# A two-layer recurrent trunk on one core: two low parts by GpSimd and a third buffer at the second layer's first sevenfold head, five low parts by accumulating DMA in the output projection's first pair

## The chip, the cores and the metric

The kernel runs on one core of a Trainium2 chip. The time is device microseconds of a whole execution. A profile is one execution that was recorded; its span runs from the first instruction to the last, and its own device time is a little longer than its span. Of the core's engines, PE multiplies matrices, DVE (VectorE), ACT (ScalarE) and POOL (GpSimd) work on rows of 128 partitions, SP issues most DMAs, and POOL issues those that add to what they write.

## What is computed

One inference step of a two-layer trunk, for a prompt of 1024 tokens and 32 sample tokens (together 1056 columns, D = 1024). Layer 0 is an RG-LRU block, layer 1 an HGRN2 block with 8 heads of 128. Cut to layer 1, on which the change works:

```
xn = _rmsnorm(x, g_norm)
u = xn @ w_in                       # 1024 x 4096: q, f, iv, gate
q, f, iv, gate = split(u, 4)
q = silu(q); log_g = log(lb + (1 - lb) * sigmoid(f)); k = 1 - exp(log_g); v = iv
o, S_T = chunked recurrence over q, k, v, log_g with state S0
o = o * rsqrt(mean(o * o) + EPS) * o_gain
y = o * silu(gate)
return x + y @ w_out, S_T           # then a final rmsnorm
```

All numbers are fp32. A product is taken on PE as three products of split operands: each number is cut into a high part `hi` (a rounded fp32r copy) and a low part `lo = x - hi`, and `hi hi + lo hi + hi lo` is summed in PSUM (lines 246, 247 and 248: one matmul each).

## The kernel before

The kernel is written as operations with reads, writes and an estimated duration, which a planner (`Flow`) puts in an order for each engine by list scheduling from both ends; each engine then runs its own list strictly in that order. So when one operation changes its engine or its estimate, the planner can reorder others near it.

**Products of layer 1.** Head 0 is projected plainly. From head 1 on (`HC = 1`), and in the output projection (`seven_out`), two output rows are computed together by a scheme of seven products (Strassen and Winograd) in place of eight: `seven(h, a, b, order)`. Each of the seven, here p1 to p7, is 24 matmuls of 264 columns: two halves x of 4 blocks of 3 matmuls (in `seven_out` 3 blocks, so 18). The string `order` is the order on PE: a digit is a product, "b" is a burst of the recurrence of the neighbouring head. The weights of the seven products come from four loaded blocks "11", "12", "21", "22" and a fifth buffer "s", combined in place by POOL (`combine`, L1467 for heads, L1677 for the output projection).

**Splitting a weight.** `split(p)` makes the high part by ACT (L1456, L1666) and the low part in one of two ways. `low` writes the negated high part by ACT (L319), and then POOL issues a DMA that adds the raw weight to it (L320). `subtract` computes raw minus high by DVE or by POOL (L333). Before, heads 1 to 6 use `low` for all seven, head 7 uses `subtract`, by POOL for p1, p2, p6, p7 and by DVE for the others, and the output projection uses `subtract` by DVE (`BYDMA` is empty). High and low parts have four buffers each (`NW = 4`), used in turn: p1 and p2 take two, the next two products of the order the other two, and a later product takes a buffer when PE has finished with it.

**Sums of x.** The seven products read x and sums of its rows. `build` makes p6, p7 and p4's sums (tiles `t2`, `t3`, `t4`, printed as `t`); `build1` makes p5's: for j = 0 to 3 it loads a row of xn (528 KB) into one of two spare buffers (`sg`, `a`), subtracts its halves (L1416), and splits the result into `xh` by ACT (L1379) and `xl` by DVE (L333). `build` also uses a third buffer, row 3 of `R`. Parts of that row hold weights of the next `seven`.

**The bursts.** Burst 3 of a head is 64 matmuls at L1061, which read rows that DVE has scaled at L1043 (`128x128x4`), and 64 at L1115, which read rows scaled next (`128x64x8`). Burst 4 reads rows scaled after those: L1139 (`128x32x16`) and L1146 (`128x16x32`). Each scaling comes in two instructions, one on `R` and one on `a` or `sg`. Burst 2 reads at L1061 rows scaled by `128x264x2`.

**Head 1 and the output projection.** Head 1's first `seven` runs in the order `FQ0`, with bursts 3 and 4 of head 0. The output projection runs four pairs of output rows, m = 0, 2, 4, 6, by `seven_out`; its operands are the sums of y (`youts`), split by ACT (L1626) and DVE (L333, tiles `xl` and `t`). Its first pair runs after head 7, whose burst 2 stands just before.

Of the kernel before, what the change touches and what calls it, by code (L numbers as in the profile page):

```python
# [24 lines left out]
NW, NXO, NRAW = 4, 3, 3  # L25
K1 = 6
NMM = 3
BYDVE, BYDMA = (1, 2, 3, 4, 5, 6, 7), ()
HC = 1
FQ0, FQ, GV = "1267b4b35", "12b675b43", "126b74b53"  # L30
SPOTS, SPOTS0 = (6, 9, 0, 2), (2, 5, -1, -1)
LAST = "12b675b43", "12b67b453", "12b675b43", "1b267543"
K2 = 8 - K1
# [7 lines left out]
TOK = SEQ + NB * NS  # L41
# [5 lines left out]
H = 8  # L47
# [167 lines left out]
def tile_trunk(ctx: ExitStack, tc: tile.TileContext, xT, prm, hc, w0, wg, wo0, w1, wo1, s_in,  # L215
               yT, h_out, c_out, sp_out, ss_out):
    nc = tc.nc
    V, S, G, T, Q = nc.vector, nc.scalar, nc.gpsimd, nc.tensor, nc.sync
# [11 lines left out]
    R = work.tile([128, 4, TOK], F32, tag="R", name="R")  # L230
# [70 lines left out]
    with ExitStack() as l0:  # L301
# [29 lines left out]
        def subtract(e, n, b, x, a, r, w, prio):  # L331

            emit = lambda: e.tensor_tensor(b, x, a.bitcast(F32), op=ALU.subtract)  # L333
            if e is G:
                pool(n, emit, r, w, prio)
            else:
                dve(n, emit, r, w, prio, True)
# [25 lines left out]
        rows = [C("sg") for _ in range(6)]  # L363
# [491 lines left out]
        raw = (halves[1][:8], [slots[i] for i in (1, 4, 7, 2, 5, 8)] + [halves[1][8], free[8]], free[:8])  # L855
# [82 lines left out]
    with ExitStack() as l1:  # L938
# [29 lines left out]
        SA = a_rows[1]  # L968
# [28 lines left out]
        def ykeys(m, a, n):  # L997

            return [("Y", m, i) for i, (u, v) in enumerate(zip(CUTS, CUTS[1:])) if u < a + n and v > a]
# [404 lines left out]

        def build1():

            spare = cycle([(rows[3], ykeys(1, 0, TOK)), (SA, [("SA", 0), ("SA", 1)])])
            for j in range(4):
                t, tk = next(spare)
                hk, lk = ([("T", 1, i, j, x) for x in range(2)] for i in (0, 1))  # L1410
                for i, ks_ in enumerate((hk, lk)):
                    for k in ks_:
                        inherit(k, [(("xh", "xl")[i], j, c) for c in (1, 2)])
                dma(t, xn[j], (), tk, 3, 528)
                t, o = t[:, :HT], t[:, HT:]
                dve(HT, lambda o=o, t=t: V.tensor_tensor(o, o, t, op=ALU.subtract), tk, tk, 3, True)  # L1416
                parted(HT, V, xh[j][:, HT:], xl[j][:, HT:], o, tk, hk, lk)
# [11 lines left out]
        def seven(h, a, b, order, at=()):  # L1429
# [24 lines left out]
            def split(p):  # L1454
                (raw, rk), (hi, hk), (lo, lk) = slot[named[p]], next(his), next(los)
                act(512, lambda: S.copy(hi, raw), (rk,), (hk,), 2)  # L1456
                if h < H - 1:
                    low(512, lo, raw, (rk,), (lk,), 2)
                else:
                    subtract(G if p in (1, 2, 6, 7) else V, 512, lo, raw, hi, (rk, hk), (lk,), 2)  # L1460
                parts[p] = hi, lo, (hk, lk)
                if p not in (1, 2):
                    freed.append(slot[named[p]])
# [28 lines left out]
            for c in order:  # L1492
# [5 lines left out]
                p = int(c)  # L1498
                if p == steps[-1]:
                    rawq = [moves.get(k, (o, k)) for o, k in freed]  # L1500
                hi, lo, wk = parts[p]
# [145 lines left out]
        def seven_out(m, order, at):  # L1647
# [15 lines left out]
            def split(p):  # L1663
                (raw, rk), (hi, hk), (lo, lk) = slot[named[p]], next(his), next(los)
                hi, lo = hi[:, :u], lo[:, :u]
                act(u, lambda: S.copy(hi, raw), (rk,), (hk,), 2)  # L1666
                if p in BYDMA:
                    low(u, lo, raw, (rk,), (lk,), 2)
                else:
                    subtract(V if p in BYDVE else G, u, lo, raw, hi, (rk, hk), (lk,), 2)  # L1670
                parts[p] = hi, lo, (hk, lk)
                if p not in (1, 2):
                    freed.append(whole[named[p]])
# [23 lines left out]
            for c in order:  # L1697
# [3 lines left out]
                p = int(c)  # L1701
                if p == steps[-1]:
                    rawq = [(o, k) for o, k in freed]
                hi, lo, wk = parts[p]
# [47 lines left out]
        for m in range(KD):  # L1752
            raw, rk = next(raws)
# [184 lines left out]
```

## Time and profile before

| | us |
|---|---|
| median of 3 runs | 1071.77 (1071.49 to 1074.11) |
| the profiled execution, its own time | 1068.75 |
| its span | 1067.0 |
| PE busy in the span | 1046.7 (98%) |
| DVE busy | 782.0 (73%) |
| ACT busy | 676.2 (63%) |
| POOL busy | 505.5 (47%) |

PE is busy in nearly all of the span, so the time is PE's work plus the little time in which it waits, or runs at a lower granted clock. The places of the change are read from PE's waits and from the order in time of DVE, ACT and POOL around them. A PE row in the order of time starts when its matmul starts, and its duration overlaps the next ones: starts of neighbours are 0.12 us apart at 264 columns.

### The profile page before, as it was taken

How to read it: one execution, taken by the hardware profiler on the slowest of the kernel's cores; microseconds unless marked ns; L12 is line 12 of the kernel's file. 1: busy time of each engine (PE TensorE's matmuls, PEld its weight loads, DVE VectorE, ACT ScalarE, POOL GpSimd, SP SyncE). 2: the span in 40 equal slices, each digit the busy share in tenths (PEclk: the TensorE clock that was granted, in tenths of full speed). 3: DMA queues.
4: the chain of work that ended last, by engine and by line, in shares of the span. 5: the costliest groups of instructions: out<-in, count | busy, mean ns of one | idle time of the engine just before them, and what ended most of it. 6: DMA issues, size and time to landing. Idle time of an engine off the chain costs nothing.

```text
span 1067.0 us, 25951 instructions
## 1 busy us (share of the span) xinstructions
PE 1046.7 (98%) x10120; PEld 1019.2 (96%) x10120; DVE 782.0 (73%) x1533; ACT 676.2 (63%) x1526; POOL 505.5 (47%) x528
## 2 busy tenths in 40 slices
PE   9999999999999999999989999999999989999997
PEld 9999999999999999999979999999999989999996
DVE  7999996888888688265786666656566576898636
ACT  6568656867765874243468685858586755865443
POOL 3425443454443456455544445455554454335354
PEclk9999999999999999999999999999999999999998
DMA  9111112124842685363685475756476652734634
GB/s 302 60 27 45 55 49 74 57 61 114 248 142 59 201 278 158 119 216 123 197 217 110 114 169 103 173 111 167 98 180 130 169 123 83 254 95 112 142 72 163
DMA packets 90331, 143.24 MB, mean 134 GB/s; under 512 B 11104, under 2 KB 55904, under 8 KB 90208
## 3 DMA queue, kind: packets, MB, share of 16 engines
q1 hardware_dynamic: 74656, 112.46, 33.2%
q0 software_dynamic: 13248, 26.35, 14.9%
q10 hardware_dynamic: 2304, 2.77, 0.8%
q8 instruction: 79, 1.29, 0.5%
q14 instruction: 44, 0.36, 0.1%
HBM read 81.60 MB, written 33.05 MB: 107 GB/s over the span
## 4 chain that ended last, share of the span: by engine, by line
PE 88%; DVE 7%; DMA 2%; ACT 1%; issue 1%; POOL 0%; POOLq 0%; ACTq 0%; SPq 0%; DVEq 0%
PE mm L246 24%; PE mm L248 24%; PE mm L247 24%; PE hg L1061 2%; PE hg L1278 1%; PE hg L577 1%; PE hg L1170 1%; PE hg L1280 1%; PE hg L1224 1%; PE hg L246 1%; PE hg L247 1%; PE hg L248 1%; DVE sg L1043 1%; DMA wlo<-wraw 1%; PE hg L1322 1%
## 5 line engine op out<-in xcount | busy, mean ns | idle before, releaser
L246 PE MATMUL mm<-xh,whi 128*128 128x352 f32 (+1 forms) x1147 | 354.7, 309 | 4.1 <-ACT os L1248 2.6
L247 PE MATMUL mm<-xl,whi 128*128 128x352 f32 (+1 forms) x1147 | 348.5, 304 | 0.0
L248 PE MATMUL mm<-xh,wlo 128*128 128x352 f32 (+1 forms) x1147 | 348.3, 304 | 0.0
L246 PEld LDWEIGHTS mm<-xh,whi 128*128 128x128 f32 x1147 | 215.5, 188 | 7.5 <-ACT os L1248 2.8
L247 PEld LDWEIGHTS mm<-xl,whi 128*128 128x128 f32 x1147 | 215.7, 188 | 1.7 <-issue 0.2
L248 PEld LDWEIGHTS mm<-xh,wlo 128*128 128x128 f32 x1147 | 215.6, 188 | 0.0
L333 POOL TENSOR_TENSOR wlo<-wraw,whi 128x512 fp32r<-128x512 f32 (+1 forms) x66 | 94.3, 1437 | 92.7 <-ACT whi L388 75.7
L248 PE MATMUL mm<-t,wlo 128*128 128x264 f32 x408 | 116.6, 286 | 3.8 <-DMA wlo<-wraw 3.8
L246 PE MATMUL mm<-t,whi 128*128 128x264 f32 x408 | 118.9, 291 | 0.0
L247 PE MATMUL mm<-t,whi 128*128 128x264 f32 x408 | 116.5, 286 | 0.0
L509 DVE SCALAR_TENSOR_TENSOR k<-xb,prm_sb,k 128x352 f32<-128x352 f32 (+2 forms) x144 | 90.1, 637 | 10.9 <-ACT k L506 6.1
L248 PEld LDWEIGHTS mm<-t,wlo 128*128 128x128 f32 x408 | 77.4, 190 | 4.2 <-DMA wlo<-wraw 4.2
L246 PEld LDWEIGHTS mm<-t,whi 128*128 128x128 f32 x408 | 77.6, 190 | 0.3
L247 PEld LDWEIGHTS mm<-t,whi 128*128 128x128 f32 x408 | 77.7, 190 | 0.1
L1540 DVE TENSOR_TENSOR k<-mm,k 128x264 f32<-128x264 f32 x72 | 30.6, 430 | 52.5 <-PE mm L248 50.4
L320 POOL DMA_DIRECT2D wlo<-wraw x51 | 44.5, 885 | 51.5 <-ACT wlo L319 35.6
L592 POOL TENSOR_TENSOR k<-X 128x352 f32<-128x352 f32 x36 | 43.8, 1226 | 47.6 <-DVE R L593 37.9
L246 PE MATMUL mm<-yh,whi 128*128 128x352 f32 x153 | 49.9, 326 | 0.0
L248 PE MATMUL mm<-yh,wlo 128*128 128x352 f32 x153 | 49.4, 323 | 0.0
L247 PE MATMUL mm<-yl,whi 128*128 128x352 f32 x153 | 49.4, 323 | 0.0
L388 ACT CAST whi<-wraw 128x512 fp32r<-128x512 f32 (+1 forms) x63 | 36.3, 591 | 20.2 <-DMA wraw<-in_w_dram 10.0
L320 POOL DMA_DIRECT2D wlo<-R x30 | 28.1, 936 | 43.1 <-ACT wlo L319 40.6
(425 smaller groups left out, 2724.2 us busy)
## 6 DMA issues: line engine op xcount, KB each, us to landing
wraw<-in_w_dram SPq DMA_DIRECT2D x88, 256.0 KB, 3.5
wlo<-wraw POOLq DMA_DIRECT2D x51, 256.0 KB, 4.0
wlo<-R POOLq DMA_DIRECT2D x30, 256.0 KB, 4.2
wraw<-in_wo_dram SPq DMA_DIRECT2D x37, 192.0 KB, 3.0
ysum<-sg SPq DMA_DIRECT2D x9, 528.0 KB, 4.0
si<-in_s_in_dram SPq DMA_DIRECT2D x8, 512.0 KB, 4.5
R<-in_w_dram SPq DMA_DIRECT2D x16, 256.0 KB, 3.3
out_ss_out_dram<-si SPq DMA_DIRECT2D x8, 512.0 KB, 2.7
```

Source lines behind the costliest of these rows:

```text
L246: T.matmul(out, wh, xh, start=first, stop=False, skip_group_check=chained)
L247: T.matmul(out, wh, xl, start=False, stop=False, skip_group_check=chained)
L248: T.matmul(out, wl, xh, start=False, stop=last, skip_group_check=chained)
L320: fl.add("POOL", 0.93, lambda: G.dma_start(dst.bitcast(F32), src, accum_op=ALU.add), (*r, *w), w, prio, n / 2)
L333: emit = lambda: e.tensor_tensor(b, x, a.bitcast(F32), op=ALU.subtract)
L388: act(m, lambda hi=hi, raw=raw, m=m: S.copy(hi[:, :m], raw[:, :m]), rk, (hk,), prio)
L509: dve(u, lambda src=src, dst=dst, sh=sh, k=k: V.scalar_tensor_tensor(dst, sh(src, k), pc("cw", 12 * k + m), dst, op0=ALU.mult, op1=ALU.add ...
L577: fl.add("PE", 0.62, lambda ps=ps, i=i, c=c: T.matmul(ps[:96, :CH], gs[:, i, :], ST[:96, chunk(c)], start=True, stop=True), (("gs",), *((" ...
L592: pool(CH, lambda x=x, a=a, b=b: G.tensor_tensor(x, a.bitcast(F32), b.bitcast(F32), op=ALU.add), (ak, bk), (xk,), 3)
L1043: dve(n // 2, lambda sv=sv, dv=dv, s=s, f=f: V.tensor_tensor(dv[:, :, s, :], sv[:, :, s, :], f, op=ALU.mult), (*sk, *gk), dk if i == o els ...
L1061: T.matmul(ps[32 * j:32 * j + 32, n * w:n * w + w], B[:, o:o + 32], q(slice(o, o + 32)), start=True, stop=True, tile_position=(0, 32 * j))
L1540: dve(QT, lambda: V.tensor_tensor(o[0], z[0], u[0], op=ALU.add), (z[1], u[1]), (o[1],), 0)
```

## The change

Head 1's first `seven` gets another order: p7 moves behind burst 3 (`FQ0`). In it, the low parts of p6 and p7 are made by POOL's subtraction in place of ACT's negated copy and POOL's adding DMA (`BYG`). `build1` gets row 3 of `R` as a third spare buffer. In the output projection's first pair (`MD = (0,)`), the low parts of p6, p7, p5, p4 and p3 are made by `low` in place of DVE's subtraction.

```diff
-BYDVE, BYDMA = (1, 2, 3, 4, 5, 6, 7), ()
+BYDVE, BYDMA, MD = (1, 2, 3, 4, 5, 6, 7), (6, 7, 5, 4, 3), (0,)
 HC = 1
-FQ0, FQ, GV = "1267b4b35", "12b675b43", "126b74b53"
+BYG = (6, 7)
+FQ0, FQ, GV = "126b74b35", "12b675b43", "126b74b53"
...
         def build1():
...
-            spare = cycle([(rows[3], ykeys(1, 0, TOK)), (SA, [("SA", 0), ("SA", 1)])])
+            spare = cycle([(rows[3], ykeys(1, 0, TOK)), (SA, [("SA", 0), ("SA", 1)]), (R[:, 3], [("R3", 0), ("R3", 1)])])
...
             def split(p):
...
-                if h < H - 1:
+                if h < H - 1 and ((h, a) != (HC, 0) or p not in BYG):
                     low(512, lo, raw, (rk,), (lk,), 2)
                 else:
-                    subtract(G if p in (1, 2, 6, 7) else V, 512, lo, raw, hi, (rk, hk), (lk,), 2)
+                    subtract(G if p in (1, 2, 6, 7) or h == HC else V, 512, lo, raw, hi, (rk, hk), (lk,), 2)
...
-                if p in BYDMA:
+                if m in MD and p in BYDMA:
                     low(u, lo, raw, (rk,), (lk,), 2)
                 else:
                     subtract(V if p in BYDVE else G, u, lo, raw, hi, (rk, hk), (lk,), 2)
```

One line is added near the top, so that line numbers of the changed kernel are one higher (L333 is L334 there). The texts name the lines of the kernel before, except in rows of the changed one.

**POOL in head 1.** This is POOL's list from the third combination of head 1's first `seven` on, before (`wraw_119` holds block "11" and then p6's weight, `wraw_120` p7's, `wraw_121` p4's, `kt_5251` p3's and later p5's; `wlo_126` and `wlo_127` are the low parts of p6 and p7):

```order
L1467 TENSOR_TENSOR wraw_119<-wraw_119,kt_5251 128x512
L1467 TENSOR_TENSOR kt_5251<-kt_5251,wraw_119 128x512
L320 DMA wlo_127<-wraw_120 128x512
L320 DMA wlo_126<-wraw_119 128x512
L320 DMA wlo_128<-wraw_121 128x512
L320 DMA wlo_129<-kt_5251 128x512
```

and the same place of the changed kernel:

```order
L1468 TENSOR_TENSOR wraw_119<-wraw_119,kt_5251 128x512
L1468 TENSOR_TENSOR kt_5251<-kt_5251,wraw_119 128x512
L334 TENSOR_TENSOR wlo_126<-wraw_119,whi_122 128x512
L334 TENSOR_TENSOR wlo_127<-wraw_120,whi_123 128x512
L321 DMA wlo_128<-wraw_121 128x512
L321 DMA wlo_129<-kt_5251 128x512
```

Two issues of adding DMAs (p7's first) are now two subtractions (p6's first), and p4's DMA stands behind them.

**DVE in head 1.** This is DVE's list from the first scaling for burst 3 on, before (`t41` is the low part of p4's sums, `sg_147`, `a_113` and row 3 of `R_73` are `build1`'s buffers, `k_85` takes sums from PSUM):

```order
L1043 TENSOR_TENSOR R_73<-R_73,sg_148 128x128x4
L1043 TENSOR_TENSOR sg_146<-sg_146,sg_148 128x128x4
L1043 TENSOR_TENSOR R_73<-R_73,sg_148 128x64x8
L333 TENSOR_TENSOR t41_5234<-a_113,t40_5233 128x1056
L1416 TENSOR_TENSOR sg_147<-sg_147 128x528
L1043 TENSOR_TENSOR a_112<-sg_146,sg_148 128x64x8
L1540 TENSOR_TENSOR k_85<-mm_156,k_85 128x264
L1540 TENSOR_TENSOR k_85<-mm_157,k_85 128x264
L333 TENSOR_TENSOR xl_94<-sg_147,xh_93 128x528
L1555 SCALAR_TENSOR_TENSOR R_73<-R_73,k_85 128x264
L1065 COPY_PREDICATED attnd_5236<-mask2_88,hg_162 128x256
L1065 COPY_PREDICATED attnd_5236<-mask4_89,hg_162 128x256
```

and in the changed kernel:

```order
L1044 TENSOR_TENSOR R_73<-R_73,sg_148 128x128x4
L1044 TENSOR_TENSOR sg_146<-sg_146,sg_148 128x128x4
L334 TENSOR_TENSOR t41_5234<-a_113,t40_5233 128x1056
L1044 TENSOR_TENSOR R_73<-R_73,sg_148 128x64x8
L1044 TENSOR_TENSOR a_112<-sg_146,sg_148 128x64x8
L1417 TENSOR_TENSOR sg_147<-sg_147 128x528
L1541 TENSOR_TENSOR k_85<-mm_156,k_85 128x264
L1044 TENSOR_TENSOR R_73<-R_73,sg_148 128x32x16
L1417 TENSOR_TENSOR R_73<-R_73 128x528
L334 TENSOR_TENSOR xl_94<-sg_147,xh_93 128x528
L1044 TENSOR_TENSOR a_112<-a_112,sg_148 128x32x16
L334 TENSOR_TENSOR xl_98<-R_73,xh_97 128x528
```

The scalings for burst 4 (`128x32x16`, and after these rows `128x16x32`) have come forward between the sums of `build1`, whose third sum now stands in `R`; the copies at L1065 and half of the sums from PSUM have gone behind them.

**DVE before the output projection.** This is DVE's list before burst 2 of head 7, before:

```order
L1043 TENSOR_TENSOR R_73<-R_73,ST_143 128x528
L1186 TENSOR_TENSOR kst_5242<-mm_156,kst_5242 32x128
L1186 TENSOR_TENSOR vst_5243<-mm_156,vst_5243 32x128
L1043 TENSOR_TENSOR a_112<-a_112,ST_143 128x528
L333 TENSOR_TENSOR xl_98<-xl_98,xh_97 128x528
L333 TENSOR_TENSOR xl_102<-xl_102,xh_101 128x528
L333 TENSOR_TENSOR xl_104<-xl_104,xh_103 128x528
L333 TENSOR_TENSOR xl_106<-xl_106,xh_105 128x528
L1043 TENSOR_TENSOR R_73<-R_73,sg_148 128x264x2
L1043 TENSOR_TENSOR sg_146<-a_112,sg_148 128x264x2
```

and in the changed kernel:

```order
L1044 TENSOR_TENSOR a_112<-a_112,ST_143 128x528
L1187 TENSOR_TENSOR kst_5242<-mm_156,kst_5242 32x128
L1187 TENSOR_TENSOR vst_5243<-mm_156,vst_5243 32x128
L1053 TENSOR_TENSOR sg_148<-ST_143 128x528
L1044 TENSOR_TENSOR R_73<-R_73,sg_148 128x264x2
L1044 TENSOR_TENSOR sg_146<-a_112,sg_148 128x264x2
L334 TENSOR_TENSOR xl_98<-xl_98,xh_97 128x528
L334 TENSOR_TENSOR xl_102<-xl_102,xh_101 128x528
L334 TENSOR_TENSOR xl_104<-xl_104,xh_103 128x528
L334 TENSOR_TENSOR xl_106<-xl_106,xh_105 128x528
```

The two scalings that burst 2 reads have moved ahead of four low parts of the sums of y.

On POOL, the five adding DMAs of the first pair stand among the combinations of its weights and two powers (L1306) of head 7's norms; on ACT, five negated copies are added in the same stretch. On SP, the load of `build1`'s third row (into `R`) stands ahead of the row for `a`, and the weight block that goes to row 3 of `R` has moved behind all four loads of `build1`.

## The prediction

> **What bounds the kernel now.** The page comes first: who is busy, and who ends the span.
>
> ```profile
> PE 1046.7 (98%) x10120; PEld 1019.2 (96%) x10120; DVE 782.0 (73%) x1533; ACT 676.2 (63%) x1526; POOL 505.5 (47%) x528
> ...
> PE 88%; DVE 7%; DMA 2%; ACT 1%; issue 1%; POOL 0%; POOLq 0%; ACTq 0%; SPq 0%; DVEq 0%
> ```
>
> PE bounds it, and the change adds and removes no matmul. So it can move the time only through PE's 20 us that are not busy, or through the granted clock. The view of PE's waits says where these are, and the windows give the clock there.
>
> ```profile
> PE mm L248 <- DMA wlo<-wraw: 3.8, 2, 3.5
> PE mm L246 <- ACT os L1248: 2.6, 1, 2.6
> PE hg L1061 <- ACT t L1626: 1.7, 1, 1.7
> ...
> 540.00:545.00 5.00, 2.16 (x18) 1.95 (x17) 5.00 (x8) 4.20 (x8) 1.71 (x3) 1.00 1.05 222
> 545.00:550.00 5.00, 4.31 (x23) 4.31 (x24) 3.31 (x8) 1.62 (x4) 0.65 (x1) 0.66 1.05 256
> 870.00:880.00 10.00, 7.25 (x176) 6.42 (x162) 8.70 (x13) 1.96 (x5) 9.40 (x9) 1.00 0.01 2
> ```
>
> The first and third waits lie in the two places of the change. The first costs more than its 3.5 us: behind it the clock column (third from the right) is 0.66 over 5 us, and 5 x 0.34 = 1.7 us of PE's work is lost on top. The second wait, in an unchanged place, cost no clock (1.00). In order of time, PE in head 1's first `seven`:
>
> ```profile
> 541.75 0.28 PE L246 MATMUL mm<-t,whi 128*128 128x264 f32 x1
> 541.88 0.28 PE L247 MATMUL mm<-t,whi 128*128 128x264 f32 x1
> 545.69 0.39 PE L248 MATMUL mm<-t,wlo 128*128 128x264 f32 x1 [3.53 <-DMA wlo<-wraw]
> ...
> 552.99 0.73 PE L1061 MATMUL hg<-R,sg 128*32 128x32 f32 x62
> 553.57 0.71 PE L1115 MATMUL hg<-R,a 128*16 128x16 f32 x62
> 554.21 0.39 PE L246 MATMUL mm<-t,whi 128*128 128x264 f32 x1
> 557.49 0.46 PE L1139 MATMUL hg<-R,a 128*32 128x32 f32 x32
> 558.78 0.69 PE L1146 MATMUL hg<-R,sg 128*64 128x64 f32 x16 [0.84 <-ACT wlo L319]
> 559.81 0.37 PE L246 MATMUL mm<-xh,whi 128*128 128x264 f32 x1
> 565.10 0.39 PE L246 MATMUL mm<-xh,whi 128*128 128x264 f32 x1 [0.37 <-DVE k L1540]
> ```
>
> At 541.75 p6 starts and at its third matmul waits for its low part. p7 follows, burst 3 (552.99), p4 (554.21), burst 4 (557.49), p3 (559.81), and p5, whose second half starts at 565.10. I compare that last moment.
>
> **Head 1: POOL's two subtractions.** Before, p6's low part was the second of these issues:
>
> ```profile
> 536.82 2.07 POOL L1467 TENSOR_TENSOR kt<-kt,wraw 128x512 f32<-128x512 f32 x1 [0.20 <-DMA wlo<-kt]
> 538.84 1.79 POOL L320 DMA_DIRECT2D wlo<-wraw  x2
> ...
> wlo<-wraw POOLq DMA_DIRECT2D x7, 256.0 KB, 4.8
> ...
> 871.55 1.27 POOL L333 TENSOR_TENSOR wlo<-wraw,whi 128x512 fp32r<-128x512 f32 x1
> 875.27 1.27 POOL L1467 TENSOR_TENSOR wraw<-wraw 128x512 f32<-128x512 f32 x1
> ...
> 871.92 5.17 DVE L1043 TENSOR_TENSOR sg<-sg 128x512 f32<-128x512 f32 x1
> ```
>
> An issue (0.9 us) and a landing (4.8) ended at 545.7. A subtraction of this very form took 1.27. POOL is free at 538.9, so p6's low part is there at 540.2, 1.8 us before PE asks, and p7's at 541.4. The 3.5 and the 1.7 us go; so do two negated copies on ACT and two transfers from a stretch whose DMA share was 1.05.
>
> What they cost falls on DVE. The last row shows it: a scaling that takes 0.69 elsewhere took 5.17, because POOL's subtractions and combinations ran without a gap from 871.55 to 876.54, and it ended 0.55 after them. DVE's list at the change, before:
>
> ```profile
> 537.66 2.35 DVE L333 TENSOR_TENSOR t<-R,t 128x1056 fp32r<-128x1056 f32 x1
> 539.98 1.26 DVE L1398 TENSOR_TENSOR a<-a,R 128x1056 f32<-128x1056 f32 x1
> 541.15 0.69 DVE L1043 TENSOR_TENSOR R<-R,sg 128x512 f32<-128x512 f32 x1
> 541.75 0.69 DVE L1043 TENSOR_TENSOR sg<-sg 128x512 f32<-128x512 f32 x1
> ...
> a<-xn SPq DMA_DIRECT2D x4, 528.0 KB, 5.5
> ...
> DMA to landing us min/median/max: 3.3/4.5/7.9
> ```
>
> The first row is 2.35 long because POOL held it until 538.9; 1.1 was left. Now POOL holds until 541.4, so it ends at 542.5, in time for p6's second half (541.75 + 12 x 0.12 = 543.2). Then, start to start, 1.2 for L1398 and 0.6 for each scaling: burst 3's first pair is ready at 544.9. `t41` (1.2) and the second pair (1.2) follow: 547.3.
>
> PE: p6 takes 24 x 0.122 = 2.9 us, to 544.65; L1061 starts at 545.0 and takes 0.6; L1115 **waits 1.8 us**, to 547.4, and ends at 548.05 (0.65, from its row to p4's). p7 and p4 end at 553.9. Burst 4 took 559.81 - 557.14 (p4's end, 554.21 + 2.93) = 2.67 with its wait of 0.84, so 1.8 without: p3 from 555.7.
>
> Is burst 4's input there? DVE after 547.3: two small steps, then scalings, sums and low parts of 0.6 in the order shown, to the last scaling at about 552.8. This needs the row of xn in `R`: its buffer is free at 543.7, and 5.5 us later, at 549.2, it has landed, just as DVE asks. L1146 asks 0.8 after burst 4 begins, at 554.7, so 1.9 us are spare; one operation of POOL fits. p5 needs the last `xl`, which stands behind p3's first half on DVE (555.7 + 1.45, then 0.45 + 0.35 + 0.6 and two hand-overs of 0.1): 558.8. Its second half starts 1.5 us later, at 560.3, against 565.10: **4.8 us gained**. The next `seven` begins earlier by the same; its first low parts now wait for PE's buffers, so they move with PE.
>
> Bounds. If POOL's three operations take 1.8 to 2.1 each, as L1467 at 536.82 did, 1.4 is lost; a landing of 7.9 (the longest of a low part's DMA there, the last row) in place of 5.5 costs 0.5 past the spare time, and some hand-overs 0.3. So 2.6 at least. With no wait at all it would be 4.8 + 1.8 + 0.4 = 7.0. I take the middle path, whose durations are rows of the same form.
>
> Of the clock: a wait of 2.6 kept 1.00 and one of 3.53 lost it, so 1.8 should keep it. The Trainium skill ("TensorE: Matmul & The Clock Gate", What's actually happening) says the clock halves after an idle window of about 3.4 us, and that the window runs free. The trace agrees. If every wait halved the clock, the sum would be 1.7 us worse.
>
> **Output projection: burst 2's wait.** PE waited 1.74 us for two scalings that stood behind four low parts:
>
> ```profile
> 932.18 0.75 PE L1061 MATMUL hg<-R,sg 128*32 128x32 f32 x64 [1.74 <-ACT t L1626]
> ...
> 927.40 3.40 DVE L333 TENSOR_TENSOR xl<-xl,xh 128x528 fp32r<-128x528 f32 x4
> 930.72 0.70 DVE L1043 TENSOR_TENSOR R<-R,sg 128x528 f32<-128x528 f32 x1
> 931.34 0.70 DVE L1043 TENSOR_TENSOR sg<-a,sg 128x528 f32<-128x528 f32 x1
> ...
> 952.13 0.39 PE L246 MATMUL mm<-t,whi 128*128 128x264 f32 x1
> 961.87 0.29 PE L246 MATMUL mm<-xh,whi 128*128 128x264 f32 x1
> ...
> 932.65 3.67 POOL L1677 TENSOR_TENSOR wraw<-wraw,R 128x384 f32<-128x384 f32 x1 [4.27 <-DVE wlo L333]
> 937.91 1.51 POOL L1677 TENSOR_TENSOR R<-R,wraw 128x384 f32<-128x384 f32 x1
> ...
> 950.00:960.00 10.00, 10.00 (x198) 9.43 (x197) 9.92 (x24) 7.05 (x25) 3.90 (x4) 1.00 0.29 81
> ...
> wlo<-wraw POOLq DMA_DIRECT2D x51, 256.0 KB, 4.0
> ```
>
> (ACT's `t` is named only because it came last; DVE's second scaling ended at 932.04.) With the four moved behind, the scalings start about 3 us earlier and end near 929, before PE's 930.4. So 1.7 goes, and the four low parts, which PE reads after 940, are hidden by p5 and p3.
>
> The five low parts themselves save DVE 5 x 0.5 us in a stretch where it is full (9.92 of 10), and cost POOL five issues of 0.9 and ACT five copies of 0.5, both with room (3.90, 7.05). Each lands 5 us after its copy: p6's near 945, and PE starts p6 (952.13 before) near 950.4. The tightest is p3's: its buffer is free when p6 ends, about 952.6, it lands near 958.5, and PE asks 1.7 earlier than 961.87, at 960.1. So they cost nothing as long as POOL comes to them. DVE's relief could also take away a later wait of 0.6 (968.09); bounds 0 to 2.3, and I take 1.7.
>
> **Sum.** 4.8 + 1.7 = 6.5 us: 1068.75 of the profiled execution becomes 1062.25. That execution was 3.0 below the median of the runs, so for the median 1071.77 - 6.5 = 1065.3.
>
> **Rivals.**
> 1. *The second gain is given back.* PE arrives at the next bursts earlier, with DVE as full as before, and waits there. For it: the row of 950 to 960. Only head 1's 4.8 is left: 1067.0.
> 2. *DVE becomes the bound in head 1.* POOL's run is longer, or the new row lands late, and burst 4 waits as well as burst 3; the gain is the lower bound of 2.6 with half of the second place, 0.9, or 1.3 less (one more operation of POOL) with none of it: 1068.3 to 1070.5. For it: the row of 5.17, and a DMA share above 1. Against it: two transfers of low parts are gone from that queue.
> 3. *Slower: POOL is starved before p6 of the first pair.* The row of 3.67 is a combination (1.27 x 384 / 512 = 1.0 alone) that waited while DVE ran without a gap. POOL's list is strict, and the adding DMAs of p6 and p7 stand behind the last such combination, which before needed no hurry. Were POOL held until 945.5, p6 would be just in time; each us later is a us of PE, and past 3.5 us the clock costs 1.7 more. From about 950 the whole gain of 6.5 is eaten, and at 955 the kernel is 4.7 slower: 1076.5. Against it: the row of 937.91, that last combination, which came through at once between DVE's operations that read PSUM. The Trainium skill speaks for it ("SBUF — State Buffer", SBUF: two separate sides): while DVE holds the port pair, POOL cannot write descriptors either. Here the row of 538.84 is against: two issues took 1.79 beside DVE's long operation.
> 4. *It doesn't do what it says*: the planner's order leaves p6 waiting. POOL's list rules it out.
>
> **How the numbers follow.** The forecast 0.62, rival 1 0.14, rival 2 0.16, rival 3 0.08. The lower end is both upper bounds, 7.0 + 2.3 = 9.3: 1062.5; the upper end takes in rival 2: 1070.5. About 0.3%, 3.2 us, is what a measurement can tell from no change: faster by more is the forecast and rival 1 (0.76), within it rival 2 (0.16), slower rival 3 (0.08).
>
> **What would show it.** Head 1: no wait on a low part at p6, a clock of 1.00 throughout, a wait of about 1.8 at L1115 for DVE's `a`, none or little at L1146, and two POOL rows of L334 near 1.3 each. Burst 2 of head 7: no wait at L1061. First pair: no wait on a DMA of `wlo`. It is wrong if L1115 or L1139 waits over 4 us, if the clock still falls, or if p6 or p3 of the first pair waits for its DMA.

## The result, and the profile after

The changed kernel takes 1065.74 us (median of 4 runs, 1063.54 to 1066.95), the kernel before, on the same chip, 1071.63 (4 runs). The ratio is 0.9955, 95% interval 0.9934 to 0.9976. A second measurement with more runs agrees: 1065.13 (12 runs) against 1069.36 (35 runs), ratio 0.9953 (0.9937 to 0.9969). So the change gains 4 to 6 us, and the forecast of 1065.3 holds. It is not made quite as forecast, as the profiles show.

The profiled execution after took 1065.36 us, span 1063.6, against 1068.75 and 1067.0 before. The profiled execution of before was 2.9 us under the median of 1071.63; that of after lies near its own. So the two profiles differ by 3.4 us where the medians differ by 5.9.

Busy times of the page after, and the view of PE's waits (us in total, times, longest):

```profile
PE 1046.8 (98%) x10120; PEld 1019.3 (96%) x10120; DVE 780.2 (73%) x1528; ACT 675.9 (64%) x1529; POOL 510.9 (48%) x533
...
PE mm L247 <- ACT os L1249: 3.0, 1, 3.0
PE hg L1116 <- DVE a L1044: 1.7, 1, 1.7
...
PE mm L249 <- issue: 0.9, 1, 0.9
...
PE mm L247 <- DVE sg L1541: 0.8, 1, 0.8
```

The wait for `wlo` (3.8) and that for `t` at L1061 (1.7) are gone. In their place stand 1.7 at L1116, as forecast, and small waits of 0.9 (at a matmul of the output projection's first p6, for which the profile names no releaser) and 0.8 (at 760 us, head 4). The windows after, with the clock third from the right:

```profile
540.00:545.00 5.00, 5.00 (x94) 4.80 (x94) 5.00 (x4) 2.34 (x4) 4.11 (x3) 1.00 0.62 184
545.00:550.00 5.00, 3.30 (x108) 3.18 (x96) 5.00 (x9) 4.52 (x10) 1.74 (x2) 0.83 0.99 235
550.00:555.00 5.00, 5.00 (x37) 4.99 (x35) 3.53 (x7) 2.64 (x6) 0.00 (x0) 0.83 1.06 265
870.00:880.00 10.00, 7.05 (x54) 6.59 (x48) 8.81 (x14) 2.19 (x5) 8.20 (x8) 0.83 0.03 8
```

p6 runs through (540 to 545: PE busy all 5 us, clock 1.00). But behind the wait of 1.7 us the clock falls: 0.83 over 10 us is 1.7 us of PE's work. It also falls behind the unchanged wait near 875 us, where before it had stayed at 1.00.

In order of time, the rows of head 1 and of head 7's burst 2 after:

```profile
537.54 2.35 DVE L334 TENSOR_TENSOR t<-R,t 128x1056 fp32r<-128x1056 f32 x1
538.72 4.58 POOL L334 TENSOR_TENSOR wlo<-wraw,whi 128x512 fp32r<-128x512 f32 x2
539.81 2.34 DVE L1399 TENSOR_TENSOR a<-a,R 128x1056 f32<-128x1056 f32 x1
542.07 1.78 DVE L1044 TENSOR_TENSOR R<-R,sg 128x512 f32<-128x512 f32 x1
...
546.15 0.68 DVE L1044 TENSOR_TENSOR a<-sg 128x512 f32<-128x512 f32 x1
546.97 0.69 PE L1116 MATMUL hg<-R,a 128*16 128x16 f32 x64 [1.70 <-DVE a L1044]
...
555.52 0.69 PE L1147 MATMUL hg<-R,sg 128*64 128x64 f32 x16
556.65 0.71 DVE L1417 TENSOR_TENSOR sg<-sg 128x528 f32<-128x528 f32 x1 [2.45 <-DMA sg<-xn]
557.28 2.15 DVE L334 TENSOR_TENSOR xl<-a,xh 128x528 fp32r<-128x528 f32 x1
559.83 0.39 PE L247 MATMUL mm<-xh,whi 128*128 128x264 f32 x1
...
926.83 1.52 DVE L1044 TENSOR_TENSOR sg<-a,sg 128x528 f32<-128x528 f32 x1
928.31 0.73 PE L1062 MATMUL hg<-R,a 128*32 128x32 f32 x62
```

POOL's two subtractions took 4.58 us, not 2.5: they did not hold DVE off in one piece, but took turns with its operations, each of which is 1.1 us longer. The second pair of scalings ended at 546.83 all the same. New is the row at 556.65: DVE waited 2.45 us for the fourth row of xn. And burst 2 (928.31) starts without a wait: its last scaling ended at 928.35, and the matmuls that read it start at 928.88.

To compare kernels, I take the start of one fixed place in each head, the first matmul of `hg<-sg,kt` behind burst 2, as a difference in us to the profiled execution of the kernel before (negative is earlier); e1 to e12 are the experiments below.

| | median (runs) | head 1 (585.6) | head 2 (642.9) | head 6 (871.0) | head 7 (932.9) | last (988.2) |
|---|---|---|---|---|---|---|
| changed, 1st profile | 1065.74 (4) | -3.53 | -4.05 | -3.12 | -3.27 | -2.32 |
| changed, 2nd profile (e4) | 1065.13 (12) | -3.59 | -4.10 | -5.23 | -4.97 | -4.85 |
| e1, head 1 part alone | 1066.88 (12) | -3.48 | -1.48 | -1.74 | -0.15 | -0.12 |
| e2, output part alone | 1067.99 (12) | -0.16 | -0.14 | 0.02 | -1.28 | -0.93 |
| e3, old order | 1069.35 (12) | -1.07 | -1.30 | -2.44 | -5.71 | -4.74 |
| e5, two buffers | 1071.93 (12) | 3.30 | 2.75 | 2.99 | 2.53 | 3.17 |
| e10, no subtractions | 1069.75 (12) | -0.01 | -0.22 | 0.84 | 4.20 | 4.53 |

The median of the kernel before, measured beside each of e1 to e12 on the same chip, was 1068.96 to 1069.40. A single profile scatters by 2 us and more behind head 1; the medians in the first column scatter less.

### The profile page after: what moved, and what is told of

Same layout as the page of the kernel before. It is cut to its first block, busy times and chain, and to the rows that moved or that the text cites. A ratio compares the mean times of both kernels' runs of the same rounds, so it can differ in the third digit from the quotient of the medians.

```text
span 1063.6 us, 25952 instructions
## 1 busy us (share of the span) xinstructions
PE 1046.8 (98%) x10120; PEld 1019.3 (96%) x10120; DVE 780.2 (73%) x1528; ACT 675.9 (64%) x1529; POOL 510.9 (48%) x533
## 4 chain that ended last, share of the span: by engine, by line
PE 87%; DVE 8%; DMA 2%; issue 1%; ACT 0%; POOL 0%; SPq 0%; POOLq 0%; ACTq 0%; DVEq 0%
PE mm L247 24%; PE mm L248 24%; PE mm L249 24%; PE hg L1062 2%; PE hg L1171 1%; PE hg L1279 1%; PE hg L578 1%; PE hg L1281 1%; DVE t L334 1%; PE hg L247 1%; PE hg L248 1%; PE hg L249 1%; PE hg L1225 1%; DVE R L1044 1%; DVE xl L334 1%
## 5 line engine op out<-in xcount | busy, mean ns | idle before, releaser
L334 POOL TENSOR_TENSOR wlo<-wraw,whi 128x512 fp32r<-128x512 f32 (+1 forms) x68 | 97.6, 1443 | 91.0 <-ACT whi L389 74.4
```

## Experiments: the two parts, and the same kernel again

**e1** makes the first pair's low parts by DVE again, **e2** puts head 1 back:

```diff
-BYDVE, BYDMA, MD = (1, 2, 3, 4, 5, 6, 7), (6, 7, 5, 4, 3), (0,)
+BYDVE, BYDMA, MD = (1, 2, 3, 4, 5, 6, 7), (6, 7, 5, 4, 3), ()
```

```diff
-BYG = (6, 7)
-FQ0, FQ, GV = "126b74b35", "12b675b43", "126b74b53"
+BYG = ()
+FQ0, FQ, GV = "1267b4b35", "12b675b43", "126b74b53"
...
-(SA, [("SA", 0), ("SA", 1)]), (R[:, 3], [("R3", 0), ("R3", 1)])])
+(SA, [("SA", 0), ("SA", 1)])])
```

> Only the head 1 part: the output projection's first pair makes its low parts by DVE's subtraction again. My theory: the two parts are independent, so head 1 shows what it showed in the changed kernel (no wait on a low part at p6, about 1.7 us at L1116, burst 4 without a wait), p5's second half 3.8 to 4.1 us earlier than in the kernel before, and burst 2 of head 7 waits about 1.7 us at L1062 again, since DVE's four low parts of y's sums stand ahead of its two scalings as before. Total: 3.5 to 4.5 us faster than before, 1.5 to 2 us slower than the changed kernel. Rival (the output projection's part gives nothing that lasts; PE arrives at the next bursts earlier and waits there): as fast as the changed kernel, 5.5 to 6 us faster than before.

> Only the output projection's part: head 1 as before (old order, adding DMAs for all low parts, two spare buffers). My theory: p6 of head 1 waits 3.5 us on its low part with 1.7 us of clock lost behind it, as before; burst 2 of head 7 does not wait, and 1.0 to 1.7 us of that reaches the end, so the kernel is 1.0 to 2.0 us faster than before. Rival (given back): the wait at burst 2 is gone, but the kernel is within 0.5 us of before, and the time shows as new waits between 930 and 1045 us.

Measured: e1 0.9965 (0.9947 to 0.9983), 2.5 us faster than before; e2 0.9985 (0.9970 to 1.0000), 1.4 us faster. Together 3.9, against 4.2 for both at once: the parts add up. Burst 2 of head 7 waits 1.74 us in e1 and not at all in e2, and in e2's profile the place behind it comes 1.28 us earlier and stays 0.93 earlier: most of the second gain lasts, which speaks against the rival (given back). The interval of e2 reaches 1.0000, so the size of this gain is loose; the changed kernel against e1, on the same chip (1065.13 and 1066.88), shows a second gain of 1.75. e1's total is an us short of the 3.5 to 4.5 that I expected, which still lies in its interval (1.8 to 5.7 us); its profile shows a loss of that kind. Behind head 1 it is 3.48 us ahead, as the changed kernel, and 2 us of that are lost at once. The rows in order of time, of e1:

```profile
583.52 0.86 POOL L321 DMA_DIRECT2D wlo<-R  x1
583.77 3.61 DVE L1044 TENSOR_TENSOR sg<-sg 128x512 f32<-128x512 f32 x1
584.12 1.57 POOL L1468 TENSOR_TENSOR wraw<-wraw,R 128x512 f32<-128x512 f32 x1
...
588.31 0.39 PE L247 MATMUL mm<-xh,whi 128*128 128x264 f32 x1 [1.42 <-ACT os L1249]
```

and of the changed kernel's second profile (e4), in which all lists are the same up to there:

```profile
583.45 0.68 DVE L1044 TENSOR_TENSOR sg<-sg 128x512 f32<-128x512 f32 x1
...
584.22 0.88 POOL L321 DMA_DIRECT2D wlo<-R  x1 [0.80 <-ACT wlo L320]
```

In the second `seven` of head 1, DVE's scaling and POOL's issue of an adding DMA come up within 0.8 us of each other. Where DVE is first, its scaling takes 0.68 us. Where POOL is first, by 0.25 us, the scaling waits through POOL's whole run and takes 3.61; ACT and PE wait behind it. In the four profiles with these lists (changed twice, e1, e11) it went each way twice; in the kernel before the scaling took 1.44. So some executions, half if four profiles are a fair sample, give back 2 us of head 1's gain here. The Trainium skill ("SBUF — State Buffer", Who interferes with whom) says that whoever issues first gets the shared ports for the whole instruction and the other fully blocks; here the one who lost waited for a run of POOL instructions, not for one.

> The changed kernel once more, for a second profile and more times. My theory: how long the granted clock stays down after a short wait depends on where the wait falls in a window that runs free of the program, so the same waits (1.7 us at L1116, about 3 us at L248 near 875 us) lose the clock in one execution and not in another, and executions of one kernel differ by 1.7 us or a multiple of it. Then this profile shows a clock of 1.00 behind at least one wait where the first profile showed less, or the other way round. Rival: the clock falls behind the same waits by the same amount each time, and the profile's clock rows agree within 0.02.

Measured: the profile of e4 (1062.9 us) shows the same wait at L1116 with another clock. Its windows (PE's busy time, then the clock):

```profile
545.00:550.00 5.00, 3.33 (x94) 1.00 1.01 231
550.00:555.00 5.00, 5.00 (x83) 1.00 1.00 283
```

and its rows in order of time:

```profile
546.75 0.69 PE L1116 MATMUL hg<-R,a 128*16 128x16 f32 x64 [1.68 <-DVE a L1044]
549.52 0.32 SPq L316 DMA_DIRECT2D sg<-xn  x1
...
556.63 0.71 DVE L1417 TENSOR_TENSOR sg<-sg 128x528 f32<-128x528 f32 x1 [3.41 <-DMA sg<-xn]
557.26 2.12 DVE L334 TENSOR_TENSOR xl<-a,xh 128x528 fp32r<-128x528 f32 x1
559.30 0.42 DVE L1541 TENSOR_TENSOR k<-mm,k 128x264 f32<-128x264 f32 x1
559.77 0.39 PE L247 MATMUL mm<-xh,whi 128*128 128x264 f32 x1 [1.83 <-DVE k L1541]
```

A wait of 1.6 to 1.7 us at L1116 lost the clock in one execution of five (the first of the changed kernel) and kept it in four (e1, e4, e6, e11); the wait of 2.6 to 3.0 near 875 us kept it in before and lost it in after. So the length of a wait does not decide alone, as my theory had it. The Trainium skill ("TensorE: Matmul & The Clock Gate", What's actually happening) says that the window of the gate runs free, which agrees. The rule on which the prediction relied, that the clock halves after an idle window of about 3.4 us, does not cover this case: the wait that lost it was 1.70 us.

More important: the lost clock cost nothing here. p5 begins at 559.83 in the first profile and at 559.77 in the second, which had 1.7 us more of clock and then waited 1.83. Something else sets p5: the fourth row of xn, loaded into `sg` when the first has been split (549.52), is there only at 556.6 (DVE idle for 3.41 us until then, and named so). Behind it in DVE's list stands the emptying of PSUM at 559.30, for which PE waits.

## Experiments: what of head 1 is needed

**e3** and **e8** put p7 back before burst 3; **e5** takes the third buffer away; **e10** makes the low parts of p6 and p7 by adding DMAs again. All keep the rest of the change.

```diff
-FQ0, FQ, GV = "126b74b35", "12b675b43", "126b74b53"
+FQ0, FQ, GV = "1267b4b35", "12b675b43", "126b74b53"
```

```diff
-            spare = cycle([(rows[3], ykeys(1, 0, TOK)), (SA, [("SA", 0), ("SA", 1)]), (R[:, 3], [("R3", 0), ("R3", 1)])])
+            spare = cycle([(rows[3], ykeys(1, 0, TOK)), (SA, [("SA", 0), ("SA", 1)])])
```

```diff
-BYG = (6, 7)
+BYG = ()
```

> The changed kernel with the old order in head 1: p7 stands before burst 3 again; POOL's subtractions and the third buffer stay. My theory: burst 3's inputs were ready 1.7 us late in the changed kernel because nothing stood between p6 and the burst; p7 (2.9 us) now hides that, so the 1.7 us wait at L1116 and the 1.7 us of clock behind it go. But POOL makes p7's low part first here, so p6's comes 1.3 to 2.3 us later and PE waits 0 to 1.6 us there. Net 1 to 3.4 us faster than the changed kernel, 7 to 9 us faster than before. Rival (DVE is the bound in this stretch, whatever the order): p4 or burst 4 waits instead, and the kernel is within 0.5 us of the changed one. Second rival (moving p7 was what made the change work): p6 waits over 3 us again for its low part, and the kernel is 2 us or more slower than the changed one.

> The kernel with the old order once more, one look. Its first profile (1063.0 us) was 6.3 us below the median of its runs (1069.35, eleven others from 1068.05 to 1072.59), so that profile cannot show why it is slow. My theory: in most executions POOL's two subtractions do not alternate with DVE's long operations but wait behind them, or DVE behind POOL, so p6's low part, the second of the two, comes 3 us or more after PE asks, and the clock falls behind that wait. Then this profile shows a wait of 3 us or more at p6 and a time of 1068 or more. Rival: p6 waits about 1 us as before and the time is near 1063, so that the first profile is like the others and the median stands on something that falls outside head 1.

> The changed kernel without the third buffer: build1's four rows of xn go through sg and a alone. My theory: the third buffer is needed now that p5 comes 3.5 us earlier. The third row can only be loaded when the first has been split (549.5 us in the second profile of the changed kernel) and the fourth when the second has been (about 554); with landings of 5.5 to 7 us the fourth row is there at 560 to 561 and its low part behind it at 562, where PE asks for it at 559 to 561. So p5 waits 1.5 to 3 us more than in the changed kernel and the total is 1.5 to 3 us above it. Rival (the buffer is only in the way: the loads share the queue with the weights, and the last row lands at the same time): within 0.7 us of the changed kernel.

> The changed kernel with adding DMAs for p6 and p7 of head 1 again; the new order and the third buffer stay. My prediction's reason (the low parts by GpSimd are the gain): p6 waits 2.5 to 3.5 us for its low part, the clock falls behind it, and the kernel is 2 to 4 us slower than the changed one. Theory after the runs so far (the last row's landing bounds this stretch, and a wait ahead of it costs only what goes past it): p6 waits 2.5 to 3.5 us, but burst 3 and p5 then wait less, since DVE is no longer held by POOL and gets to the rows earlier; p5's second half is within 1 us of the changed kernel's, and the kernel within 1 us of it.

Measured: e3 0.9999 (0.9980 to 1.0018), e5 1.0017 (1.0003 to 1.0031), e10 1.0007 (0.9993 to 1.0022) of the kernel before; e8 1069.83 in its one execution. With e2 at 0.9985, each of the three parts of head 1, taken out alone, costs more than head 1's whole gain: 4.2 us for the order, 6.8 for the buffer, about 5 for the subtractions. They work only together.

*The order.* My theory of a faster kernel fell. The rival that DVE is the bound had the place right (burst 4 waits instead), but not the time: it allowed 0.5 us, and the kernel is 4.2 slower than the changed one. PE's waits in head 1 of e3, in order of time:

```profile
542.60 0.39 PE L249 MATMUL mm<-t,wlo 128*128 128x264 f32 x1 [1.05 <-POOL wlo L334]
...
553.20 0.46 PE L1140 MATMUL hg<-R,a 128*32 128x32 f32 x32 [0.44 <-DVE a L1044]
555.12 0.69 PE L1147 MATMUL hg<-R,sg 128*64 128x64 f32 x16 [1.46 <-DVE sg L1044]
562.55 0.39 PE L247 MATMUL mm<-xh,whi 128*128 128x264 f32 x1 [1.67 <-DVE k L1541]
```

L1116 waits no more, but burst 4 and p5 do, since the planner put a scaling ahead of DVE's sums and the sums, and with them the loads into the buffers they free, come later. Head 1 ends 2.5 us behind the changed kernel's. e8 shows the same four waits (0.96, 0.96, 1.46, 1.41) and not the 3 us at p6 that I expected. One head later it is 2.7 us behind e3 (644.26 against 641.55), in the race in which e1 lost its 2: POOL's issue came 0.19 us ahead of the scaling, which took 3.70 us; in e3, whose profiled execution was the fastest of twelve, it came 0.34 behind, and the scaling took 0.68.

Most of the rest of the 6.8 us between the two profiles falls in head 6, in a place that no run here changes. It is the scaling whose 5.17 us the prediction showed at 871.92. In 13 of the 14 profiles it takes 5.1 to 8.6 us beside POOL's subtractions and combinations, and PE waits 2.6 to 6.1 us behind it, the wait near 875 us. In e3 it came at 869.49, before POOL's subtraction (871.13), took 0.78, and PE waits only 1.02 us there: from the place in head 6 to that in head 7, e3 needs 58.6 us and e8 61.8. So e3's last two columns are luck of the same kind as in head 1, and the changed kernel keeps a wait of 3 us there (2.95 and 2.85 in its two profiles) that none of these runs went after.

*The buffer.* In e5, PE waits three times from 559.7 us on, 0.96, 2.25 and 2.21 us: the sums of x come too late. That is the theory, at more than twice the price I gave (1.5 to 3 above the changed kernel; 6.8 measured).

*The subtractions.* In order of time in e10, and its windows of the clock:

```profile
547.64 0.59 PE L249 MATMUL mm<-t,wlo 128*128 128x264 f32 x1 [5.26 <-DMA wlo<-wraw]
```

```profile
545.00:550.00 5.00, 2.36 (x10) 0.50 1.06 199
550.00:555.00 5.00, 5.00 (x155) 0.88 1.00 313
```

p6 waits 5.26 us for its adding DMA, 1.7 more than in the kernel before, and the clock falls to 0.50. The transfer itself was as usual (4.1 to 6.4 us); but POOL came to the three issues at 542.03, against 538.84 before, since a combination at 535.73, beside DVE's work, took 4.09 us. Behind p6 no wait of 0.25 us or more follows until 763 us: the later waits did give way, as my newer theory had it, but not by as much as the first wait costs. The profiled execution was 3 us above e10's median, and in head 6 it had the longest of the waits near 875 us (6.06), so its last two columns are no price of the subtractions; and whether the 4.09 us are typical is open. The price of about 5 us rests on the medians. The prediction's own reason was the right one.

## Experiments: the last row of xn

**e7** lets the planner expect the last row later; **e9** loads all rows in halves into the places of their own high and low parts, without waiting for a buffer; **e12** adds to e9 subtractions for p1 and p2 and the old order.

```diff
-                dma(t, xn[j], (), tk, 3, 528)
+                dma(t, xn[j], (), tk, 3, 528 if j < 3 else 1056)
```

```diff
-                dma(t, xn[j], (), tk, 3, 528)
-                t, o = t[:, :HT], t[:, HT:]
-                dve(HT, lambda o=o, t=t: V.tensor_tensor(o, o, t, op=ALU.subtract), tk, tk, 3, True)
-                parted(HT, V, xh[j][:, HT:], xl[j][:, HT:], o, tk, hk, lk)
+                dma(f(hi), xn[j][:, :HT], (), hk, 3, 264)
+                dma(f(lo), xn[j][:, HT:], (), lk, 3, 264)
+                o, ok = next(sums)
+                dve(HT, lambda hi=hi, lo=lo, o=o: V.tensor_tensor(o, f(lo), f(hi), op=ALU.subtract), (*hk, *lk), ok, 3, True)
+                parted(HT, V, hi, lo, o, ok, hk, lk)
```

```diff
-BYG = (6, 7)
-FQ0, FQ, GV = "126b74b35", "12b675b43", "126b74b53"
+BYG = (1, 2, 6, 7)
+FQ0, FQ, GV = "1267b4b35", "12b675b43", "126b74b53"
```

> The changed kernel with one number changed: the planner counts the last row of xn in build1 as 1056 KB, so it expects it later. On DVE that moves t41 behind the second pair of scalings for burst 3, and the split of the row in a, with one more copy of drained sums, ahead of the sum of the last row. In the second profile of the changed kernel, DVE waited 3.41 us for that row with a drain of PSUM behind it, for which PE then waited 1.83 us at p5; and L1116 waited 1.68 us for a scaling that stood behind t41 (1.2 us). My theory: L1116's wait falls to 0.3 to 0.8 us, with less danger for the clock, and p5's wait falls to under 1 us, so p5's second half comes 1 to 2.5 us earlier and the kernel is 0.7 to 2.5 us faster than the changed one. Rival (the row's landing itself is the bound): p5 waits as long in another place, and the kernel is within 0.5 us of the changed one.

> The changed kernel, but build1's four rows of xn are loaded in two halves straight into the places of xh and xl that their high and low parts will take (free since head 0's plain products), and the sum goes to a new half-row buffer and to row 3 of R in turn. No row waits for a buffer any more, so all four are loaded before p1 ends. My theory: the last row's landing (556.6 us in both profiles of the changed kernel, with DVE idle for 2.45 and 3.41 us before it) is what bounds p5, and through it the whole second layer. Without it p5's wait (1.83 us) goes and L1116's falls below 1.2 us, since one of the sums has moved ahead on DVE; p5's second half comes 1.5 to 3 us earlier and the kernel is 1 to 3 us faster than the changed one. Rival (eight more loads ahead of the sums' own row on the same queue): the row for t41 or the weights of the next pair come late, PE waits as long elsewhere, and the kernel is within 0.7 us of the changed one or slower.

> What the runs so far ask for, put together: the rows of xn loaded in place as in the kernel before this one (there PE had no wait between 541 and 589 us, but waited 3.54 us at p1 for a low part whose adding DMA took 8.4 us to land beside the eight loads, against 3.6 us in the changed kernel), the low parts of p1 and p2 of head 1 by GpSimd's subtraction too, so that no adding DMA stands in that crowd, and the old order, in which p7 (2.9 us) hides burst 3's late scalings. My theory: no wait of more than 1.2 us on PE from 531 to 565 us, p5's second half 2 to 3.5 us earlier than in the changed kernel, and the kernel 1.5 to 3.5 us faster than it (near 1062 where the changed one is near 1065). Rival (four subtractions of GpSimd beside DVE, and the sums' row late behind the loads, make DVE the bound): burst 3 or p6 waits 2 us or more for DVE, and the kernel is within 0.7 us of the changed one or slower.

Measured: e7 1065.55 (6 runs; 0.9957, 0.9940 to 0.9974), the same as the changed kernel: L1116's wait falls to 1.10, but then PE waits 1.11, 0.99 and 0.57 us, at three places between 557 and 563. The rival held.

e9 1068.37 (0.9990, 0.9971 to 1.0010). In its profile PE has no wait from 541 to 589 us: those at L1116 (1.68 in e4) and p5 (1.83) are gone. But it waits earlier, at p1. In order of time, and from the view of DMAs (us to landing, the adding DMAs of p1 and p2), of e9:

```profile
539.57 0.59 PE L249 MATMUL mm<-xh,wlo 128*128 128x264 f32 x1 [3.54 <-DMA wlo<-wraw]
```

```profile
wlo<-wraw POOLq DMA_DIRECT2D x1, 256.0 KB, 8.4
wlo<-kt POOLq DMA_DIRECT2D x1, 256.0 KB, 10.0
```

against, in the changed kernel (e4):

```profile
wlo<-wraw POOLq DMA_DIRECT2D x1, 256.0 KB, 3.6
wlo<-kt POOLq DMA_DIRECT2D x1, 256.0 KB, 4.6
```

Eight loads more at 526 to 531 us slow the adding DMAs from 3.6 to 8.4 us, and the wait is paid there: 3.54 us and 1.4 more of clock (0.72 from 540 to 545). Head 1 still ends only 1.2 us behind the changed kernel: of the 4.9 lost, 3.7 came back through the two waits that vanished. DVE's last sum of a row starts at 555.35 there and no row of xn is waited for from 544 on, which agrees with the late row as the bound of p5. But a PE that comes 4.9 us late would have found the rest ready anyway, so e9 cannot settle it; that the row sets p5 rests on the rows of e4.

e12 1069.90 (1.0007, 0.9993 to 1.0021): no adding DMA is late any more, and now the weights of the second `seven` come early too, so that POOL's combinations, silent from 548.2 to 555.4 in e4, run into DVE's scalings for burst 4:

```profile
551.15 2.34 DVE L1044 TENSOR_TENSOR a<-a,sg 128x512 f32<-128x512 f32 x1
551.28 1.64 POOL L1470 TENSOR_TENSOR R<-wraw 128x512 f32<-128x512 f32 x1
553.00 1.62 POOL L1470 TENSOR_TENSOR wraw<-wraw 128x512 f32<-128x512 f32 x1
553.41 1.78 DVE L334 TENSOR_TENSOR xl<-R,xh 128x528 fp32r<-128x528 f32 x1
555.11 1.75 DVE L1044 TENSOR_TENSOR R<-R,sg 128x512 f32<-128x512 f32 x1
...
557.61 1.12 PE L1147 MATMUL hg<-R,sg 128*64 128x64 f32 x16 [3.60 <-DVE sg L1044]
```

Each operation of DVE is 1.1 to 1.7 us longer than its 0.68, burst 4 waits 3.60 us, and the clock falls (0.63 from 555 to 560). The stretch has three bounds close together, the queues, DVE and PE's own order, and each repair meets the next one. No kernel tried beats the changed one; e7 and e11 equal it.

## Experiments: the order behind the second gain

**e6** keeps DVE's subtractions in the first pair and makes the four low parts of y's sums wait, in the planner, for burst 2's scalings; **e11** gives only p6 and p7 to adding DMAs.

```diff
-BYDVE, BYDMA, MD = (1, 2, 3, 4, 5, 6, 7), (6, 7, 5, 4, 3), (0,)
+BYDVE, BYDMA, MD = (1, 2, 3, 4, 5, 6, 7), (6, 7, 5, 4, 3), ()
...
             scale(h, 2, 1, 0)
+            if h == H - 1:
+                for n, row in enumerate((arow, brow)):
+                    fl.writer["mark", n] = fl.writer[row(h, 0)[1][0]]
...
-                subtract(YSUB[j], HT, lo, lo.bitcast(F32), hi, (hk, lk), (lk,), 2)
+                mark = ("mark", 0), ("mark", 1)
+                subtract(YSUB[j], HT, lo, lo.bitcast(F32), hi, (hk, lk, *(mark if p == 2 or (p, j) == (1, 2) else ())), (lk,), 2)
```

```diff
-BYDVE, BYDMA, MD = (1, 2, 3, 4, 5, 6, 7), (6, 7, 5, 4, 3), (0,)
+BYDVE, BYDMA, MD = (1, 2, 3, 4, 5, 6, 7), (6, 7), (0,)
```

> The head 1 part as in the changed kernel, and of the other part nothing but the order on DVE: the output projection's first pair keeps DVE's subtractions, but the planner is told that four low parts of y's sums come after the two scalings that burst 2 of head 7 reads. My theory: the second gain is the order alone, so this kernel has no wait at L1062 near 930 us and is 1.0 to 1.7 us faster than the kernel with the head 1 part alone, as fast as the changed kernel within 0.7 us. Rival (DVE's relief by 2.5 us counts): burst 2's wait goes, but PE waits again 0.6 us or more for DVE between 935 and 970 us, and the kernel is 1 us or more slower than the changed one.

> The changed kernel with only two of the five low parts of the first pair (p6 and p7) by adding DMA, the other three by DVE. In DVE's list, two of the four low parts of y's sums then stand ahead of the two scalings that burst 2 of head 7 reads (four in the kernel before, none in the changed one). My theory: the wait at L1062 is these low parts' time, about 0.85 us each (3.38 / 4) less 1.2 us of spare time in the changed kernel: 0.3 to 0.7 us here, against 1.74 with four and none with none; the kernel is within 1 us of the changed one. Rival (what counts is how much work DVE has in the whole stretch): no wait at L1062, but new waits for DVE of 1 us or more between 935 and 970 us.

Measured: e11 1064.45 (0.9960, 0.9946 to 0.9974), and its burst 2 waits as worked out:

```profile
928.86 0.75 PE L1062 MATMUL hg<-R,sg 128*32 128x32 f32 x64 [0.51 <-ACT t L1627]
```

1.74 with four low parts ahead, 0.51 with two, none with none, with DVE relieved of 0, 1 and 2.5 us. All subtractions of which DVE is relieved stand behind burst 2 in its list, so the relief does not act on this wait directly: the place of the low parts in the list sets it. e6 does not show the same by itself: 1071.51 (1.0014, 0.9997 to 1.0032), with these waits:

```profile
933.19 0.75 PE L1062 MATMUL hg<-R,sg 128*32 128x32 f32 x64 [1.53 <-DVE sg L1044]
...
941.70 0.39 PE L247 MATMUL mm<-xh,whi 128*128 128x264 f32 x1 [3.30 <-DVE attns L1069]
```

The scalings stand ahead there too, but the planner also put four more low parts (`t`) before the copies of `attns`, DVE came to the scalings later, and took turns with POOL at them. That kernel is no clean test: it leaves open whether the order alone, in an otherwise unchanged list, would do. What it shows is that an order forced on the planner is paid elsewhere as long as DVE keeps the five subtractions.

## Why the prediction was right, point by point

- **p6's wait and the clock behind it.** Right, and by the reason given: the wait for its low part is gone in all profiles with the subtractions in the new order (about 1 us with the old one, e3 and e8), back at 5.26 us without them (e10).
- **POOL and DVE at 538.7 to 546.8.** The sum was right within half a microsecond (second pair ready at 546.83, forecast 547.3; DVE came to this place 0.12 us and PE 0.30 us earlier than before). The way was not: I took DVE to be held until POOL had finished, from the row of 5.17 us; they took turns.
- **The wait at L1115 (L1116 after): 1.8 us.** 1.70 measured.
- **"A wait of 2.6 kept 1.00 and one of 3.53 lost it, so 1.8 should keep it."** Wrong as a rule: of five such waits one lost the clock, in the very execution profiled first, so that a sign the prediction gave of being wrong (the clock still falls) showed there. It cost nothing, since p5 was bound otherwise.
- **Burst 4 without a wait.** Right (555.52, no wait).
- **"p5 needs the last `xl` ... 558.8. Its second half starts 1.5 us later, at 560.3, against 565.10: 4.8 us gained."** This is the term that was too large. In the first profile p5 begins at 559.83, so that its second half comes at 561.3: 3.8 us; at the head's end 3.5. I followed the third row, in `R`, through its buffer and its landing, but not the fourth: it can be loaded only when `sg` has been split, and took 7.1 us to land (549.52 to 556.6) with the DMA engines full. Then POOL's combination held the split of `a` for 2.15. So the rows of e4 have it; e9 agrees without proving it. The 2.6 to 7.0 of the bounds held it.
- **"The next `seven` begins earlier by the same."** Only in some executions. In two of the four profiles with these lists, 2 us of it were lost in the race of DVE's scaling with POOL's issue near 583.6. No term stood for this.
- **Burst 2, 1.7 us.** Right at its place; 1.28 us of it had reached PE's next place in e2, and 1.4 the end. The five adding DMAs were not waited for by name. Ahead of a matmul of p6 stand 0.7 to 1.0 us without a named releaser in six profiles with all five (after, e3, e8, e9, e10, e12), 0.5 in e5, 0.2 in e2, and none in e4 and e7. In the first profile it is the matmul at 951.60, and PE had read p6's low part from 949.78 on, so its DMA had landed; what the wait is for stays open.
- **Rivals.** 1 (second gain given back) is spoken against by e2 and by the changed kernel against e1. 2 (DVE the bound in head 1) was partly so: not at burst 4, but at p5, at 1.0 to 1.3 us instead of its 2.2 and more. 3 (POOL starved before p6 of the first pair) fell: the last combination there took 1.02 us.

The total: forecast 6.5, measured 5.9 against the first median and 4.2 in the larger sample, so 0.6 to 2.3 too large. The terms above account for that: 1.0 to 1.3 at p5, and 2 us in perhaps half of the executions. Measured alone, the parts bring 2.5 and 1.4, each below its term of 4.8 and 1.7, and the first the more so. The time itself came out closer than the gain because the changed kernel stayed where it was (1065.74, then 1065.13), while the kernel before came out at 1071.63, then 1069.36: the median on which 1065.3 was built was high. So that the forecast came within 0.4 us of the first median is luck: a base 2.4 us too high and a gain 2.3 us too large cancel.

## What to carry to other kernels

When a wait is removed, follow every transfer that the next stage needs back to the moment when its buffer comes free, the last one of a chain above all: a wait in front may be covering it. Parts of a change that look like alternatives (an order, a buffer, another engine) may be worth nothing but together, so take each out alone before dropping one. And where two engines that hold each other come up within a microsecond, count the price as a chance, not as a yes or no.

## What the runs showed of the hardware

- The same wait of PE (1.6 to 1.7 us) lost the granted clock in one execution of five: 0.50 to 0.66 in the 1 us windows behind it, about 3.4 us long, 1.7 us of work.
- In six profiles (e1, e6, e8, e9, e11, e12) POOL's issue of an adding DMA began 0.2 to 0.5 us ahead of a DVE scaling, with a combination directly behind the issue, and the scaling took 2.3 to 3.7 us; in three (after, e3, e4) the issue began 0.1 to 0.8 us behind it, and the scaling took 0.68. The issue alone does not hold DVE: in e7 it also began 0.25 us ahead (583.76), but the next combination came only at 585.68, and the scaling took 0.68. At 538.7 to 543.3 of the changed kernel the two took turns instead, with DVE's operations each 1.1 us longer; what decides between the two ways is open.
- Adding DMAs beside eight plain loads landed in 8.4 and 10.0 us instead of 3.6 and 4.6, issued at the same place in the program.
